# A hybrid attention step on one core: token tiles loaded first, constants on ScalarE's queue, the first chunks' high part straight from PSUM, and another order of modulation, turns and squares

## The chip, the core and the metric

One core of a Trainium2 chip runs the whole step as one program. Its engines are TensorE (PE; its weight loads are listed apart as PEld), VectorE (DVE), ScalarE (ACT), GpSimd (POOL) and SyncE (SP), each with its own queue of instructions that it works off in order; SP and ACT also issue the DMAs used here. The metric is the device time of one execution in microseconds. The kernel before takes 723.14 us, the median of three runs (722.96 to 723.36).

## What is computed

One layer of a diffusion backbone, for 128 context tokens and 1024 latent tokens of width 1024. Two attention branches (A global, B windowed) read one input projection; the change touches only what stands ahead of that projection: the modulated norm.

```python
shift, scale, gate = modulation(c, w_mod[l], b_mod[l])        # silu(c) @ w_mod + b_mod, split in three
h = rmsnorm(xs, norm_gain[l]) * (1.0 + scale) + shift          # 1024 latent tokens x 1024 columns
q_a, k_a, v_a, g_a, q_b, k_b, v_b, g_b = project(h, w_in[l], ...)
...
xs = xs + gate * merge_out(o_a, g_a, o_b, g_b, w_out[l])
```

The context tokens go the same way with a conditioning vector of their own (`c_ctx`).

## The kernel before

The projection needs h with its 1024 columns on the partitions, so h is made transposed, in eight **chunks** j of 128 columns. Nine token tiles of 128 rows (`xn`, tile 0 the context, 1 to 8 the latent tokens) are loaded by `load_x`, normed by `norm` (ACT squares and sums the tile, POOL makes `msx` and its power -1/2 `rsx`, DVE scales the tile by it in `scaled`), and turned on PE against the identity into a PSUM bank `px`. Two vectors per chunk, `a_mod` and `b_col`, hold scale and shift. They come from `modulate_rows(j)`: eight products of the Silu of the conditioning with the chunk's modulation weights `wm` (1 MB, three buffers, `load_wm`), copied out of PSUM as `mrows`; and `modulate(j)`: two turns of `mrows`, a reduction `m`, and two small operations on DVE. ACT then makes `hf` = px * a_mod + b_col (L401).

All products run in float32r with every operand split in a high and a low part: `h_at(0, ...)` is the rounded value of hf, made by a cast on DVE (L406), `h_at(1, ...)` is hf minus it, made on POOL (L407). The weights of the input projection are split alike by `split`: `whi` is cast on ACT (L233), `wlo` subtracted on DVE (L235), on POOL for every second chunk of the gate weights of branch B only. A product is high x high, high x low (`gate_high`, L262 and L263) and low x high (L258).

The first thing projected is branch A's gate (`W_GA`, raw chunks `rawga`, three buffers). Over tokens 1 to 4 (`first_gates`, four banks of 512 columns, one for each channel group ch) and 5 and 6 (`next_gates`, 256 columns, one chunk behind), the products run while the later chunks of h are still being made: the loop `for j in range(KT + 2)` makes chunk j and multiplies chunk j-1. Its pass j=0 is the opening: warm-up matmuls (`warm(n)`, a product of the identity with no use, n from `WARM`), the norms of tiles 1 to 6, the modulation of chunk 0. Tiles 7, 8 and 0 follow in the passes j=1 to 4.

The order of the work is the order of the source: at the end `in_order` chains every engine's instructions as written. PSUM banks for the turns alternate between two (`bank_tr`, tags D and E): the rows of a modulation and the transposes of a chunk take turns on them. Two engines that read the same bank are put one after the other. DMAs rotate over eight semaphores, so that an issue waits until the DMA issued eight places earlier has landed; a raw weight buffer is loaded again when its split is done, a `wm` buffer when its products are.

Of the kernel before, what the change touches and what calls it, by code (L numbers as in the profile page):

```python
# [18 lines left out]
P = 128  # L19
D = 1024  # L20
# [35 lines left out]
PAD = 2  # L56
X_FROM = 1
SECOND_FROM = 5
WARM = (8, 4, 4, 2)
WIDE = 5  # L60
LOADLEAD = 5
OUTRATE = 2.5
PADRATE = 3
POOL_LO = ("gb",)
NOG = 5
PES = 3
GATE_LATE = 2
# [40 lines left out]
def hybrid_step(ctx, tc, x_prompt, x_sample, cache_k_a, cache_v_a, cache_k_b, cache_v_b,  # L108
# [97 lines left out]
    class Weights:  # L206
# [22 lines left out]
        def split(self):  # L229
            k = len(self.hi)  # L230
            h = wp.tile([P, 512], F32R, tag="whi", name=f"whi{self.tag}_{k}")
            l = wp.tile([P, 512], F32R, tag="wlo", name=f"wlo{self.tag}_{k}")
            nc.scalar.copy(h, self.raw[k])  # L233
            eng = nc.gpsimd if self.tag in POOL_LO and k % 2 else nc.vector
            eng.tensor_tensor(l, self.raw[k], h, op=ALU.subtract)  # L235
            self.hi.append(h)
            self.lo.append(l)
            self.load()
# [71 lines left out]
    FIRST = [1, 2, 3, 4, 5, 6]  # L310
    with tc.tile_pool(name="st", bufs=2, side="right") as st:
        ident = st.tile([P, P], F32, name="ident", bufs=1)
        nc.sync.dma_start(ident, k_ident)
        nc.vector.tensor_copy(ident_r, ident)
        nc.vector.tensor_copy(ident_b, ident)
        nc.gpsimd.tensor_copy(diag, ident[0:4, 0:4])
        colt = st.tile([P, 48], F32, name="colt", bufs=1)
        nc.sync.dma_start(colt, cols)
        st.tile([P, 16], F32, name="pad3", bufs=1)

        def group_sum(out, eye):
            nc.vector.tensor_tensor(out, eye[:, 0:2], eye[:, 32:34], op=ALU.add)
            for a in (64, 96):
                nc.vector.tensor_tensor(out, out, eye[:, a : a + 2], op=ALU.add)

        wm = []

        def load_wm(j):
            w = st.tile([P, KT, 2, P], F32, tag="wm", name=f"wm{j}", bufs=3)
            nc.sync.dma_start(w, w_mod_ss[j])  # L330
# [15 lines left out]
        def modulate_rows(j):  # L346
            pm = pmod[j] = bank_tr(f"pm{j}")
            for k in range(KT):
                a = 32 * (k % 4)
                nc.tensor.matmul(pm[a : a + 32, 0:256], sil32[:, k, :], wm[j][:, k].rearrange("p s n -> p (s n)"),  # L350
                                 start=(k < 4), stop=(k >= 4), tile_position=(0, a))
            mrows[j] = st.tile([P, 256], F32, tag="mrows", name=f"mrows{j}")
            (nc.scalar.copy if j else nc.vector.tensor_copy)(mrows[j], pm[:, 0:256])

        def modulate(j):
            pm = pmod.pop(j)[:, 256:512]
# [6 lines left out]
            nc.vector.tensor_scalar(a_mod[:, j, :], m4[:, 0], bsc1[:, j : j + 1], colt[:, 16 + j : 17 + j],  # L363
                                    op0=ALU.add, op1=ALU.mult)
            nc.vector.tensor_scalar(b_col[:, j, :], m4[:, 1], colt[:, 24 + j : 25 + j], None, op0=ALU.add)

        xn = {}

        def load_x(t):
            xn[t] = st.tile([P, D], F32, name=f"xn{t}", bufs=1)  # L370
            nc.sync.dma_start(xn[t], x_tile[t])

        rx = {}

# [3 lines left out]
        def norm(t, now_=True):  # L378
# [10 lines left out]
            else:  # L389
                rx[t] = r  # L390

        def transposed(j, t0, n, cond):
            px = bank_tr(f"px{j}_{t0}")
            for i in range(n):
                if j == 0 and t0 == 1:
                    warm(WARM[3])
                nc.tensor.transpose(px[:, P * i : P * i + P], xn[t0 + i][:, P * j : P * j + P], ident)
# [3 lines left out]
            nc.scalar.activation(hf[:, :w], px[:, :w], AF.Identity,  # L401
                                 scale=a_mod[:, j, cond : cond + 1], bias=b_col[:, j, cond : cond + 1])
            step = w if third(dst) else 2 * P
            for o in range(0, w, step):
                i, to = third(slice(dst.start + o, dst.start + o + step))
                nc.vector.tensor_copy(h_at(0, i, j, to), hf[:, o : o + step])  # L406
                nc.gpsimd.tensor_tensor(h_at(1, i, j, to), hf[:, o : o + step], h_at(0, i, j, to), op=ALU.subtract)  # L407

        for t in FIRST[:4]:
            load_x(t)  # L410
        W_GA.load()
        load_x(5)
        load_x(6)
        load_wm(1)
        W_GA.load()
        load_wm(2)
        def warm(n):

            for _ in range(n):
                nc.tensor.matmul(small[0], ident_b, ident_b.unsqueeze(1).to_broadcast([P, 4, P]), start=True, stop=True)  # L420
# [19 lines left out]

        for j in range(KT + 2):
            if j == 0:
                warm(WARM[0])
                norm(1)
                modulate_rows(0)
                warm(WARM[1])
                norm(2)
                modulate(0)
                warm(WARM[2])
                norm(3)  # L450
                norm(4)
# [23 lines left out]
            if big_on:  # L475
                first_gates(2, j - 1)
            if j < KT:
                modulate(j)
                transposed(j, 1, 4, 0)
            if big_on:  # L480
                first_gates(3, j - 1)
            if j < KT:
                transposed(j, 5, 2 if j < WIDE else 4, 0)
# [839 lines left out]
```

## Time and profile before

| what | value |
|---|---|
| median of three runs | 723.14 us |
| the profiled execution: span from first to last instruction | 721.3 us |
| the median's part outside such a span | 1.84 us |
| granted TensorE clock, mean over the span | 0.993 |
| PE idle in the span (721.3 - 698.3 busy) | 23.0 us |
| DMA: bytes moved, mean | 78.56 MB, 109 GB/s |

The time of the profiled execution beside its span isn't recorded; the span and the median are set side by side here. Times in all rows are microseconds from the start of the span; a row of the timeline gives start, duration, engine, line, operation, output and inputs, count, and in brackets the idle time of the engine ahead of it with what ended it. A row of a stretch gives its length, then the busy time of PE, PEld, DVE, ACT and POOL with the number of instructions, the granted clock, the DMA engines' busy share and GB/s. A stretch asked for PE alone has PE's busy time alone. SPq and ACTq are the DMA issues of SP and ACT.

### The profile page before, as it was taken

Reading aid. Unit: us, or ns where it says so; the run is one execution under the profiler, and the core shown is the slowest. Engines: PE = TensorE matmul, PEld = TensorE weight load, DVE = VectorE, ACT = ScalarE, POOL = GpSimd, SP = SyncE. Lnnn points to the kernel's source line nnn. Section 1 sums busy time; section 2 is a strip of 40 time slices with the busy share of each in tenths; the row PEclk is TensorE's granted clock in tenths of the full one; section 3 lists DMA queues with packets and bytes.
Section 4 is the critical chain, followed back from the end, with each engine's and each line's share of the span. In section 5 each row is a group of like instructions: output and inputs, shape, how many; then the busy total and the mean of one; then the engine's idle time right before and its main releaser. Section 6 shows DMA issues by size and latency. Waiting matters only on the chain. (4 is left out here: it accounts for less than half of the span.)

```text
span 721.3 us, 10622 instructions
## 1 busy us (share of the span) xinstructions
PE 698.3 (97%) x3524; PEld 559.7 (78%) x3524; DVE 457.6 (63%) x1007; ACT 411.7 (57%) x829; POOL 335.3 (46%) x355
## 2 busy tenths in 40 slices
PE   5999999999999999999999999999999999999997
PEld 2678988877777788977788888888888888887865
DVE  3466147875675872745866677577666775775653
ACT  5355411411232451158778877877787778877770
POOL 3456013332322340236666555655575557555751
PEclk9999999999999999999999999999999999999999
DMA  8961373348435115440321222121212221212323
GB/s 344 346 219 59 121 278 86 79 94 276 121 85 142 45 60 171 139 143 23 103 67 45 73 67 88 44 81 52 87 54 59 66 87 45 81 53 87 103 65 119
DMA packets 53159, 78.56 MB, mean 109 GB/s; under 512 B 6569, under 2 KB 25449, under 8 KB 52081
## 3 DMA queue, kind: packets, MB, share of 16 engines
q1 hardware_dynamic: 44928, 65.96, 28.1%
q10 hardware_dynamic: 8176, 11.94, 6.3%
q8 instruction: 28, 0.46, 0.3%
q14 instruction: 27, 0.21, 0.1%
HBM read 58.69 MB, written 19.18 MB: 108 GB/s over the span
## 5 line engine op out<-in xcount | busy, mean ns | idle before, releaser
L1108 POOL TENSOR_TENSOR pl<-pe,ph 128x512 fp32r<-128x512 f32 x130 | 167.6, 1292 | 144.7 <-DVE nm L919 67.5
L859 DVE TENSOR_REDUCE mx<-pmx 128x1 f32<-128x384 f32 x192 | 101.4, 552 | 59.5 <-PE pmx L858 58.1
L1100 ACT ACTIVATE pe<-st 128x512 f32<-128x512 f32 x146 | 86.8, 594 | 28.0 <-PE st L1098 27.1
L1104 ACT CAST ph<-pe 128x512 fp32r<-128x512 f32 x146 | 90.6, 621 | 4.8
L1118 PE MATMUL pv<-ph,v_hi 128*128 128x512 f32 x208 | 83.2, 400 | 2.2 <-DVE spare L1142 2.2
L1121 PE MATMUL pv<-pl,v_hi 128*128 128x512 f32 x208 | 82.6, 397 | 0.0
L173 POOL TENSOR_TENSOR rs_q<-ms_q,mhalf 128x8 f32<-128x8 f32 x18 | 34.8, 1931 | 82.1 <-DVE ms_q L171 82.1
L1189 PE MATMUL po<-wo,ogh 128*128 128x512 f32 x216 | 72.5, 394 | 0.2 <-DVE yt L1196 0.2
L919 DVE CUSTOM_DVE_ANT_0 sn<-sn,mask,nsink 128x512 f32<-128x512 f32 (+1 forms) x64 | 46.3, 724 | 38.3 <-PE sn L916 36.5
L858 PE MATMUL pmx<-kha,qt 128*128 128x384 f32 x192 | 61.0, 363 | 0.4 <-ACT pen L905 0.2
L1097 PE MATMUL st<-qt,kha 128*128 128x512 f32 x144 | 58.3, 405 | 1.5 <-ACT pe L1100 0.8
L1098 PE MATMUL st<-qb,kla 68*128 68x512 f32 x144 | 57.6, 400 | 1.1 <-DVE qb L878 1.1
L1120 PE MATMUL pv<-ph,v_lo 128*64 128x512 f32 x146 | 57.9, 396 | 0.0
L1121 PEld LDWEIGHTS pv<-pl,v_hi 128*128 128x128 f32 x208 | 39.4, 189 | 16.7 <-issue 0.2
L905 ACT ACTIVATE pen<-sn,nm 128x512 f32<-128x512 f32 (+2 forms) x72 | 45.0, 626 | 6.5 <-DVE nm L919 3.1
L1093 ACT CAST ph<-st 128x512 fp32r<-128x512 f32 x62 | 36.4, 587 | 19.9 <-PE st L1092 18.7
L1118 PEld LDWEIGHTS pv<-ph,v_hi 128*128 128x128 f32 x208 | 39.4, 189 | 10.5 <-ACT ogh L1154 2.4
L1189 PEld LDWEIGHTS po<-wo,ogh 128*128 128x128 f32 x216 | 40.0, 188 | 6.8 <-DVE yt L1196 0.6
L1094 DVE TENSOR_TENSOR pl<-st,ph 128x512 fp32r<-128x512 f32 x62 | 42.5, 686 | 2.3 <-ACT ph L1093 1.5
L1189 PE MATMUL po<-wo,ogl 128*128 128x512 f32 x108 | 42.6, 394 | 0.0
L594 ACT ACTIVATE sqq<-pq 128x512 f32<-128x512 f32 x18 | 10.8, 599 | 53.3 <-DMA qd<-qo0q 14.4
L858 PEld LDWEIGHTS pmx<-kha,qt 128*128 128x128 f32 x192 | 35.5, 190 | 6.2 <-DVE mx L859 1.4
(216 smaller groups left out, 1700.2 us busy)
## 6 DMA issues: line engine op xcount, KB each, us to landing
qt<-qd SPq DMA_DIRECT2D x36, 256.0 KB, 3.1
wm<-in_w_mod_ss_dram SPq DMA_DIRECT2D x8, 1024.0 KB, 5.1
qd<-qo0q ACTq DMA_DIRECT2D x36, 128.0 KB, 2.4
qd<-qo1q ACTq DMA_DIRECT2D x36, 128.0 KB, 2.4
sgl<-gd SPq DMA_DIRECT2D x36, 128.0 KB, 2.1
out_dram<-yt SPq DMA_DIRECT2D x17, 256.0 KB, 2.1
xn<-in_x_sample_dram SPq DMA_DIRECT2D x8, 512.0 KB, 7.0
wg<-in_w_mod_g_dram SPq DMA_DIRECT2D x4, 1024.0 KB, 7.9
```

The costliest lines, as they stand in the source:

```text
L858: nc.tensor.matmul(pm[:, 0:384], lhs, kha[:, g, 3 * b : 3 * b + 3, :], start=True, stop=True)
L859: nc.vector.tensor_reduce(mx[:, h, b : b + 1], pm[:, 0:384], axis=AX.X, op=ALU.max)
L919: nc.vector.tensor_tensor_reduce(s, s, mask[:, m0 : m0 + n], -1.0, nsink[:, 4 * g + h : 4 * g + h + 1], op0=ALU.add, op1=ALU.min, accum_ou ...
L1097: nc.tensor.matmul(s, kh, qtile[i], start=True, stop=False)
L1098: nc.tensor.matmul(s, kl, qbtile[i], start=False, stop=True)
L1100: nc.scalar.activation(pe, s, AF.Exp)
L1104: nc.scalar.copy(ph, pe)
L1108: nc.gpsimd.tensor_tensor(pl, pe, ph, op=ALU.subtract)
L1118: nc.tensor.matmul(pv, two, ph, start=(b == 0), stop=False)
L1120: nc.tensor.matmul(pv[0:64, :], vl, ph, start=False, stop=False)
L1121: nc.tensor.matmul(pv, two, pl, start=False, stop=last)
L1189: nc.tensor.matmul(po[n], a, wo_parts[KT * n + k][lo], start=(k == KS[0] and p == 0), stop=(k == KS[-1] and p == 2))
```

## The change

- ident and colt (the conditioning, the gain and the biases) are issued from ACT's queue, and SP starts with the four token tiles, then wm0 in two halves, the first weights, wm1, the second weights, tiles 5 and 6, wm2.
- The opening turns each of the four tiles into the bank of chunk 0 as soon as it is scaled, with warm-up matmuls between, and only then does chunk 0's modulation; `turned` and `modulated` are the two halves of the old `transposed`.
- For chunks 0 and 1 of tokens 1 to 4, ACT writes the high part straight from PSUM (L412 of the kernel after), DVE makes hf from the same bank (L413) and the low part (L414); the cast on DVE and the subtraction on POOL are gone there.
- The low part of the first weight chunk is subtracted on POOL (`POOL_FIRST`), the copied rows of chunk 1 on DVE instead of ACT.
- Tiles 5 and 6 are squared in pass 1 instead of the opening, and scaled later; their transposes of chunks 0 and 1 share one bank in pass 2. In pass 1 the modulation stands ahead of the products of ch 2 and 3, in pass 2 the order is changed as the diff shows. From pass 3 on the order is the old one.

```diff
-WARM = (8, 4, 4, 2)
+WARM = (7, 4, 5, 4, 2, 8)
+POOL_FIRST = (("ga", 0),)
...
-            eng = nc.gpsimd if self.tag in POOL_LO and k % 2 else nc.vector
+            eng = nc.gpsimd if (self.tag in POOL_LO and k % 2) or (self.tag, k) in POOL_FIRST else nc.vector
...
-        nc.sync.dma_start(ident, k_ident)
+        nc.scalar.dma_start(ident, k_ident)
...
-        nc.sync.dma_start(colt, cols)
+        nc.scalar.dma_start(colt, cols)
...
+        for t in FIRST[:4]:
+            load_x(t)
         wm = []
 
         def load_wm(j):
             w = st.tile([P, KT, 2, P], F32, tag="wm", name=f"wm{j}", bufs=3)
-            nc.sync.dma_start(w, w_mod_ss[j])
+            for a in range(0, KT, KT if j else KT // 2):
+                b = a + (KT if j else KT // 2)
+                nc.sync.dma_start(w[:, a:b], w_mod_ss[j][:, a:b])
             wm.append(w)
 
-        load_wm(0)
...
-            (nc.scalar.copy if j else nc.vector.tensor_copy)(mrows[j], pm[:, 0:256])
+            (nc.scalar.copy if j > 1 else nc.vector.tensor_copy)(mrows[j], pm[:, 0:256])
...
+        def turned(px, j, t):
+            nc.tensor.transpose(px, xn[t][:, P * j : P * j + P], ident)
...
+        def modulated(px, j, t0, n, cond):
             w = P * n
             dst = slice(P * place(t0), P * place(t0) + w)
             hf = st.tile([P, 512], F32, tag="hf", name=f"hf{j}_{t0}", bufs=3)
-            nc.scalar.activation(hf[:, :w], px[:, :w], AF.Identity,
-                                 scale=a_mod[:, j, cond : cond + 1], bias=b_col[:, j, cond : cond + 1])
+            a, b = a_mod[:, j, cond : cond + 1], b_col[:, j, cond : cond + 1]
+            if j < 2 and t0 == 1:
+                i, to = third(dst)
+                nc.scalar.activation(h_at(0, i, j, to), px[:, :w], AF.Identity, scale=a, bias=b)
+                nc.vector.tensor_scalar(hf[:, :w], px[:, :w], a, b, op0=ALU.mult, op1=ALU.add)
+                nc.vector.tensor_tensor(h_at(1, i, j, to), hf[:, :w], h_at(0, i, j, to), op=ALU.subtract)
+                return
+            nc.scalar.activation(hf[:, :w], px[:, :w], AF.Identity, scale=a, bias=b)
...
-        for t in FIRST[:4]:
-            load_x(t)
+        load_wm(0)
+        W_GA.load()
+        load_wm(1)
         W_GA.load()
         load_x(5)
         load_x(6)
-        load_wm(1)
-        W_GA.load()
         load_wm(2)
...
             if j == 0:
-                warm(WARM[0])
-                norm(1)
+                px = bank_tr("px0_1")
+                for i in range(4):
+                    norm(1 + i)
+                    warm(WARM[i])
+                    turned(px[:, P * i : P * i + P], 0, 1 + i)
                 modulate_rows(0)
-                warm(WARM[1])
-                norm(2)
+                W_GA.split()
+                warm(WARM[4])
                 modulate(0)
-                warm(WARM[2])
-                norm(3)
-                norm(4)
-                W_GA.split()
-                norm(5)
-                transposed(0, 1, 4, 0)
-                norm(6)
-                load_wm(3)
+                modulated(px, 0, 1, 4, 0)
+                warm(WARM[5])
                 continue
             big_on, small_on = j <= KT, 2 <= j
             if j < KT:
                 W_GA.split()
+            if j == 1:
+                load_wm(3)
+                norm(5, False)
...
             if j == 1:
-                transposed(0, 5, 2, 0)
+                modulate(1)
+                scaled(5, rx.pop(5))
+                transposed(1, 1, 4, 0)
+                norm(6, False)
+                first_gates(2, 0)
+                first_gates(3, 0)
+            elif j == 2:
+                scaled(6, rx.pop(6))
+                px5 = bank_tr("px01_5")
+                for i in range(4):
+                    turned(px5[:, P * i : P * i + P], i // 2, 5 + i % 2)
+                modulate(2)
+                for i in range(2):
+                    modulated(px5[:, 256 * i : 256 * i + 256], i, 5, 2, 0)
+                first_gates(2, 1)
+                transposed(2, 1, 4, 0)
+                first_gates(3, 1)
+                transposed(2, 5, 2, 0)
+            else:
```

SP's queue at the start of the program, before:

```order
L313 DMA ident<-in_k_ident_dram 128x128
L318 DMA colt<-in_cols_dram 128x48
L330 DMA wm_169<-in_w_mod_ss_dram 128x2048
L371 DMA xn_178<-in_x_sample_dram 128x1024
L371 DMA xn_180<-in_x_sample_dram 128x1024
L371 DMA xn_182<-in_x_sample_dram 128x1024
L371 DMA xn_184<-in_x_sample_dram 128x1024
L221 DMA rawga_186<-in_w_in_dram 128x512
L371 DMA xn_188<-in_x_sample_dram 128x1024
```

and now:

```order
L331 DMA xn_169<-in_x_sample_dram 128x1024
L331 DMA xn_171<-in_x_sample_dram 128x1024
L331 DMA xn_173<-in_x_sample_dram 128x1024
L331 DMA xn_175<-in_x_sample_dram 128x1024
L341 DMA wm_184<-in_w_mod_ss_dram 128x1024 x2
L222 DMA rawga_187<-in_w_in_dram 128x512
L341 DMA wm_189<-in_w_mod_ss_dram 128x2048
L222 DMA rawga_191<-in_w_in_dram 128x512
L331 DMA xn_193<-in_x_sample_dram 128x1024
L331 DMA xn_195<-in_x_sample_dram 128x1024
```

The tiles moved ahead of 1 MB of modulation weights, the constants left this queue, and tiles 5 and 6 moved behind wm1 and the second weights.

ACT's queue from the square of the fourth tile (`sq`) to the high part of chunk 1, before:

```order
L382 ACTIVATE sq_261,ss_262<-xn_184 128x1024
L233 CAST whiga_269<-rawga_186 128x512
L382 ACTIVATE sq_275,ss_276<-xn_188 128x1024
L401 ACTIVATE hf_1_296<-px_1_283,b_col,a_mod 128x512
L382 ACTIVATE sq_300,ss_301<-xn_190 128x1024
L233 CAST whiga_310<-rawga_194 128x512
L353 COPY mrows_329<-pm_320 128x256
L401 ACTIVATE hf_5_340<-px_5_337,b_col,a_mod 128x256
L401 ACTIVATE hf_1_358<-px_1_353,b_col,a_mod 128x512
```

and now, up to the copied rows of chunk 2:

```order
L386 ACTIVATE sq_249,ss_250<-xn_175 128x1024
L234 CAST whiga_273<-rawga_187 128x512
L412 ACTIVATE h_0_0_115<-px_1_205,b_col,a_mod 128x512
L234 CAST whiga_299<-rawga_191 128x512
L386 ACTIVATE sq_307,ss_308<-xn_193 128x1024
L412 ACTIVATE h_0_1_116<-px_1_342,b_col,a_mod 128x512
L386 ACTIVATE sq_351,ss_352<-xn_195 128x1024
L234 CAST whiga_364<-rawga_277 128x512
L363 COPY mrows_383<-pm_374 128x256
```

The squares of tiles 5 and 6 moved from ahead of the two activations to behind each of them; that of tile 6 stands ahead of the cast of the third weights.

DVE's queue from the last scaled tile of the opening to the split of the second weights, before:

```order
L376 TENSOR_SCALAR xn_184<-xn_184,rsx_266 128x1024
L235 TENSOR_TENSOR wloga_270<-rawga_186,whiga_269 128x512
L376 TENSOR_SCALAR xn_188<-xn_188,rsx_280 128x1024
L406 CAST h_0_0_115<-hf_1_296 128x512
L376 TENSOR_SCALAR xn_190<-xn_190,rsx_305 128x1024
L235 TENSOR_TENSOR wloga_311<-rawga_194,whiga_310 128x512
```

and now, up to the scaling of tile 6:

```order
L414 TENSOR_TENSOR h_0_0_123<-hf_1_287,h_0_0_115 128x512
L236 TENSOR_TENSOR wloga_300<-rawga_191,whiga_299 128x512
L363 COPY mrows_327<-pm_318 128x256
L371 TENSOR_REDUCE m_1_337<-pm_318 128x4
L373 TENSOR_SCALAR a_mod<-m_1_337,bsc_178,colt 128x2
L375 TENSOR_SCALAR b_col<-m_1_337,colt 128x2
L380 TENSOR_SCALAR xn_193<-xn_193,rsx_312 128x1024
L413 TENSOR_SCALAR hf_1_347<-px_1_342,a_mod,b_col 128x512
L414 TENSOR_TENSOR h_0_1_124<-hf_1_347,h_0_1_116 128x512
L236 TENSOR_TENSOR wloga_365<-rawga_277,whiga_364 128x512
L380 TENSOR_SCALAR xn_195<-xn_195,rsx_356 128x1024
```

The low part of the first weights left the queue, the low parts of the first two chunks came in, and tile 6 is scaled behind the split of the third weights.

More of the change, by code (lines that the diff above doesn't have):

```diff
@@ L324, in group_sum, with load_x @@
                 nc.vector.tensor_tensor(out, out, eye[:, a : a + 2], op=ALU.add)
+        xn = {}
+        def load_x(t):
+            xn[t] = st.tile([P, D], F32, name=f"xn{t}", bufs=1)
+            nc.sync.dma_start(xn[t], x_tile[t])
+        for t in FIRST[:4]:
+            load_x(t)
         wm = []
@@ L365, in modulate @@
             nc.vector.tensor_scalar(b_col[:, j, :], m4[:, 1], colt[:, 24 + j : 25 + j], None, op0=ALU.add)
[L367 to L371, printed above, removed]
         rx = {}
@@ L394, in transposed @@
             for i in range(n):
-                if j == 0 and t0 == 1:
-                    warm(WARM[3])
-                nc.tensor.transpose(px[:, P * i : P * i + P], xn[t0 + i][:, P * j : P * j + P], ident)
+                turned(px[:, P * i : P * i + P], j, t0 + i)
+            modulated(px, j, t0, n, cond)
+        def modulated(px, j, t0, n, cond):
             w = P * n
@@ L473, in hybrid_step @@
             if j == 1:
-                transposed(0, 5, 2, 0)
[L475 to L483, printed above, removed]
+                modulate(1)
[17 more added lines that the diff above has]
+            else:
+                if big_on:
+                    first_gates(2, j - 1)
+                if j < KT:
+                    modulate(j)
+                    transposed(j, 1, 4, 0)
+                if big_on:
+                    first_gates(3, j - 1)
+                if j < KT:
+                    transposed(j, 5, 2 if j < WIDE else 4, 0)
             if X_FROM + 1 < j <= X_FROM + 4:
```

## The prediction

> **What bounds the kernel now.** I read the page's busy table and slices first, then the stretches of the first 40 us, the waits of those stretches, and the timeline around each wait.
>
> ```profile
> PE 698.3 (97%) x3524; PEld 559.7 (78%) x3524; DVE 457.6 (63%) x1007; ACT 411.7 (57%) x829; POOL 335.3 (46%) x355
> 0.00:17.47 17.47, 10.14 (x46) 3.78 (x46) 6.61 (x16) 9.51 (x16) 6.13 (x16) 1.00 0.87 341
> 31.60:37.90 6.30, 6.30 (x51) 4.82 (x50) 2.58 (x7) 3.16 (x7) 3.16 (x5) 1.00 0.81 292
> 25.30 0.50 PE L262 MATMUL pg_f<-h,whiga 128*128 128x512 f32 x1 [0.42 <-DVE h L406]
> 31.69 0.40 PE L262 MATMUL pg_f<-h,whiga 128*128 128x512 f32 x1
> 37.99 0.40 PE L262 MATMUL pg_f<-h,whiga 128*128 128x512 f32 x1
> ```
>
> PE is busy 97% of the span, and from the third chunk (j=3, first product at 31.69) a chunk is 6.30 us of PE work in 6.30 us. So an edit ahead of 31.69 is worth just the amount by which that product comes sooner; nothing behind it is edited. Ahead of it lie 17.47 us before the first real product, chunk one (17.47 to 25.30, 7.83 us) and chunk two (25.30 to 31.69, 6.39 us). These three numbers are what I recompute.
>
> ```profile
> 6.72 0.33 SPq L330 DMA_DIRECT2D wm<-in_w_mod_ss_dram  x1
> 8.00 0.33 SPq L221 DMA_DIRECT2D rawga<-in_w_in_dram  x1
> 11.77 0.33 SPq L330 DMA_DIRECT2D wm<-in_w_mod_ss_dram  x1
> 8.00 1.06 ACT L382 ACTIVATE sq<-xn 128x1024 bf16<-128x1024 f32 x1 [4.51 <-DMA xn<-in_x_sample_dram]
> 10.12 0.75 DVE L376 TENSOR_SCALAR xn<-xn,rsx 128x1024 f32<-128x1024 f32 x1 [6.35 <-POOL rsx L386]
> 11.79 1.06 ACT L382 ACTIVATE sq<-xn 128x1024 bf16<-128x1024 f32 x1
> 15.35 0.33 PE L397 MATMUL px<-ident,xn 128*128 128x128 f32 x1 [0.70 <-DVE xn L376]
> 15.71 0.78 ACT L401 ACTIVATE hf<-px,b_col,a_mod 128x512 f32<-128x512 f32 x1 [0.86 <-PE px L397]
> 17.00 0.42 DVE L406 CAST h<-hf 128x512 fp32r<-128x512 f32 x1
> 17.47 0.50 PE L262 MATMUL pg_f<-h,whiga 128*128 128x512 f32 x1 [1.80 <-DVE h L406]
> ```
>
> The first product hangs on the loads: SP issues a load only when the one eight places earlier has landed, so its rows date the landings. The first modulation weights (wm0, 1 MB) land near 6.7, the first token tile at 8.00, the fourth at 11.77: 1.26 us per 512 KB tile. ACT squares each tile as it lands; the fourth takes 11.79 to 15.35 to reach its transpose, and then hf on ACT, the cast on DVE, the product.
>
> **The change, step by step.** *Loads.* The token tiles now stand ahead of wm0 and their first issue moves to where ident's was.
>
> ```profile
> 0.72 0.40 SPq L313 DMA_DIRECT2D ident<-in_k_ident_dram  x1
> 1.64 0.42 SPq L330 DMA_DIRECT2D wm<-in_w_mod_ss_dram  x1
> 3.33 3.60 PE L420 MATMUL pg_s<-ident_b 128*128 128x512 bf16 x8 [3.33 <-DVE ident_b L315]
> ```
>
> The fourth tile loses 1 MB ahead of it (2 x 1.26 = 2.5 us) and starts 0.92 earlier, less about 0.2 for the 88 KB of ident and colt that now share the first microseconds: 11.77 - 3.25 = 8.5; the first lands at 8.5 - 3 x 1.26 = 4.7. By the same rate wm0 lands at 11.0, the first weight chunk 11.6, wm1 14.2, tiles five and six 16.1 and 17.3, wm2 19.9, the third weight chunk 20.5. ACT issues ident at the time SP did; its table load then ends near 2.9, and the Silu it delays is wanted only by wm0's products.
>
> *Transposes.* At before's pace (11.79 to 15.35) the fourth tile could be transposed at 12.1, the first at 4.7 + 2.87 + 0.1 = 7.7. But the warm-up matmuls stand in PE's queue between them, 7, 4, 5, 4, and here the clock decides.
>
> ```profile
> 1.87:5.29 3.42, 1.96 (x5) 1.00 0.78 246
> 5.29:8.70 3.41, 3.41 (x20) 1.00 1.00 406
> 18.94:22.35 3.41, 3.41 (x22) 0.50 1.02 423
> 8.72 1.04 PE L420 MATMUL pg_s<-ident_b 128*128 128x512 bf16 x4
> 18.59 1.66 PE L350 MATMUL pm<-wm,sil 128*32 128x256 f32 x16
> 26.42 1.07 PE L350 MATMUL pm<-wm,sil 128*32 128x256 f32 x16
> ```
>
> The granted clock is 0.50 from 18.94 to 22.35, a window of 3.41 us. The column says 1.00 at the start, yet the first eight warm-up matmuls take 3.60 us (0.43 each) against about 0.22 each in the row at 8.72. I read PE as slow until 8.70, a window edge: the window before it was busy throughout, the one before that for 1.96 of 3.42 (57%) and brought no release. Now the seven first ones end at 3.33 + 3.0 = 6.35 and PE idles until 7.7, so the window to 8.70 is busy 2.1 of 3.41, 62%. That row is unknown between 57% (no release) and 100% (release). Nearest is 57%, so I take no release at 8.70 but at 12.11. At 0.43 each, four end at 9.5, five at 11.75, and one slow and three fast at about 12.95; the fourth transpose runs there, not at 12.1. With release at 8.70 this 0.9 us is not paid.
>
> *Modulation moved behind the transposes.* It was hidden under the loads; now it is on the path.
>
> ```profile
> 10.79 0.42 DVE L353 COPY mrows<-pm 128x256 f32<-128x256 f32 x1
> 11.26 0.44 PE L359 MATMUL pm<-ident,mrows 128*128 128x128 f32 x2 [1.50 <-DVE mrows L353]
> 29.18 0.17 DVE L361 TENSOR_REDUCE m<-pm 128x4 f32<-128x16 f32 x1 [1.81 <-PE pm L359]
> 29.58 0.22 DVE L365 TENSOR_SCALAR b_col<-m,colt 128x2 f32<-128x2 f32 x1
> 29.92 1.23 ACT L401 ACTIVATE hf<-px,b_col,a_mod 128x512 f32<-128x512 f32 x2 [1.99 <-DVE b_col L365]
> ```
>
> From 13.1: products 1.07, copy 0.42, turns 0.44, reduce to b_col 0.62, ACT's activation 0.78 (now writing the high part itself), with 0.05 to 0.1 between: 16.7. Eight fast warm-ups behind the turns (15.1) end at 16.85, so **the first product comes at 16.85, 0.6 sooner**. DVE's cast (17.00 to 17.42 before, half a microsecond behind ACT's end at 16.49) is gone from this path. The low weight part goes to POOL: 1.29 us by the row below, from 12.3, done by 13.6, hidden.
>
> *Chunk one.* The kernel before had 3.41 us of it at half clock (1.7 lost), turned tiles five and six in it (four transposes, 0.45), and ended in the wait of 0.42 at 25.30.
>
> ```profile
> 17.50 1.29 POOL L407 TENSOR_TENSOR h<-hf,h 128x512 fp32r<-128x512 f32 x1 [1.20 <-DVE h L406]
> 33.72 0.72 PE L258 MATMUL pg_f<-h,whiga 128*128 128x512 f32 x2
> 35.20 0.60 PE L397 MATMUL px<-ident,xn 128*128 128x128 f32 x4
> L1094 DVE TENSOR_TENSOR pl<-st,ph 128x512 fp32r<-128x512 f32 x62 | 42.5, 686 | 2.3 <-ACT ph L1093 1.5
> ```
>
> Now hf from PSUM and the subtraction run on DVE behind ACT's read of the same bank: twice 0.69 by the row of L1094 (bounds 0.42, the cast, and 1.29, POOL). They end 1.4 us after the first product could start, while PE has 2.0 us of products (31.69 to 33.72) ahead of the low part: hidden. wm1's products take the bank that hf is read from; they come 1.03 in, DVE's read ends 0.5 in: hidden too, by half a microsecond. By the steady rows the chunk is 2.03 to the low products, 0.5 for them, 0.1 of waiting for the copied rows, 0.2 turns, 0.35 transposes, 1.4 for channels two and three: 4.6. Its successor needs the next high part at 2.85 + 0.1 + 0.62 + 0.1 + 0.78 + 0.1 = 4.55. I take 4.65, **3.2 less than 7.83**. PE is nearly idle-free from 12.95 on, so I see no reason for half clock.
>
> *Chunk two.* It gains four transposes (10 instead of 6, 0.45) and a new wait: ACT squares tile six, then casts weights, DVE splits them and only then scales tile six.
>
> ```profile
> 20.40 0.69 DVE L235 TENSOR_TENSOR wloga<-rawga,whiga 128x512 fp32r<-128x512 f32 x1
> 18.01 0.62 ACT L233 CAST whiga<-rawga 128x512 fp32r<-128x512 f32 x1 [0.48 <-DMA rawga<-in_w_in_dram]
> ```
>
> From the high part at chunk start -0.2: square 1.25, cast 0.62, split 0.69, scale 0.75, small gaps: 3.1 in; PE wants tile six at 2.6. So 0.5 of waiting; behind it stand all the products of the chunk. With 6.30: 7.25, **0.86 more than 6.39**. The chunk starts at 21.5, wants wm2 at 22.5 (lands 19.9) and the third weights at 22.6 (20.5): two microseconds of cover; if that goes, every further microsecond is paid. Other moved issues: wm3 waits for wm0's release at 14.2 and lands near 24, wanted at 30.
>
> Sum: -0.62 - 3.18 + 0.86 = -2.94. Span 721.3 - 2.9 = 718.4; the median, 723.14, has 1.84 outside the span, which stays: **720.2**.
>
> **Rivals.** *The clock comes at 8.70.* Then the fourth transpose is at 12.1 and everything behind it 0.9 to 1.0 sooner: 719.2. For it: 62% lies above 57%. Against: the one window here that met the slow clock with less than full work released nothing. The page "TensorE: Matmul & The Clock Gate" of the Trainium skill (Part 1) says that these windows run freely and do not start with the kernel; the trace's 3.41 us spacing agrees, and by that rule the release could fall elsewhere in each run, though the three times before lie within 0.40 us.
>
> *POOL is not ready.* Between its memset and its first mean, POOL has an instruction without a row (a reload of its library, one place ahead of the mean in both kernels).
>
> ```profile
> 2.82 0.30 POOL L342 MEMSET sil<- 128x256 f32 x1
> 9.24 0.19 POOL L384 TENSOR_SCALAR msx<-ss 128x1 f32<-128x1 f32 x1 [6.12 <-ACT sq L382]
> 10.53 0.39 POOL L384 TENSOR_SCALAR msx<-ss 128x1 f32<-128x1 f32 x1 [0.45 <-ACT sq L382]
> 11.00 0.56 POOL L386 TENSOR_TENSOR rsx<-msx,mhalf 128x1 f32<-128x1 f32 x1
> ```
>
> It lasts anything from nothing to 6.1 us, for the first mean started 0.09 after ACT's accumulator was read. Before, nothing needed POOL sooner; now ACT delivers at 6.0, so a load over 2.9 us is paid. At 6.1: first mean 9.2, four pairs of 1.03 end at 13.3, the first transpose at 10.9 after 4.5 us of idle PE; nine slow warm-ups reach 15.0, release at 15.53, fourth transpose 16.3, first product 20.1: 723.5. Released a window later (18.94), about 1.6 more with slow products: 725.1. Against it: the first mean follows ACT as promptly as the second (0.08), which a load ending just then would do only by chance. The Trainium skill's "GPSIMD Engine Reference" (2.1 Instruction dispatch) gives about 6 us for the first call into freshly loaded code, with no visible instruction; by that figure the load would end at 9.07, an estimate that this trace neither shows nor excludes, and the kernel would be the slower one.
>
> *The gain is handed back.* Loads over two microseconds later than the rows' rate, or another window at half clock further on (1.7 us), give 721.9 to 722.5. *The change does next to nothing*: modulation, 3.6 us, now stands behind the transposes. If the tiles came only 1.6 us sooner, the first product would be at 17.6, and if PE then met a half-clock window again (1.7), the gain would be -0.1 + 3.2 - 1.7 - 0.86 = 0.5: 722.6. The loads' rate and the eight warm-ups speak against it.
>
> **How the numbers follow.** Forecast 0.43 (719.7 to 720.9), early clock 0.27, handed back 0.13, nothing 0.05, POOL 0.12. The range leaves out POOL and some of the rest: 718.7 to 722.3. About 0.2%, 1.45 us, is what a measurement can tell from no change. Faster than 721.7: forecast, early clock and part of the third, 0.77. Within: 0.16, with POOL's mild half. Slower: 0.07.
>
> **What would show it.** Right: fourth transpose near 13, first product near 16.9, no 0.50 window before 30, third chunk's first product near 28.7, a wait of PE for xn in chunk two. Early clock: warm-ups of 0.22 from 8.70. Wrong: POOL's first mean much later than ACT's first square, or weights landing after 22.6.

## The result and the profile after

| | before | after |
|---|---|---|
| median, 20 runs of each | 723.14 us (721.93 to 726.99) | 721.65 us (721.15 to 723.39) |
| ratio | | 0.9976, 95% interval 0.9967 to 0.9985 |
| profiled execution: span, mean granted clock | 721.3 us, 0.993 | 720.4 us, 1.000 |
| first product of chunk one | 17.47 | 18.41 (forecast 16.85) |
| first product of chunk two | 25.30 | 23.25 (forecast 21.5) |
| first product of chunk three | 31.69 | 30.75 (forecast 28.75) |

The kernel after is 1.49 us faster, 0.24%; the forecast was 2.94. The profiled execution of after took 722.6 us, so it is one of the slower of the twenty, by 0.95 over their median. That has to be kept in mind with every row below.

The page of the kernel after: its span, and busy time by engine with the number of instructions.

```profile
span 720.4 us, 10635 instructions
PE 698.1 (97%) x3530; PEld 558.6 (78%) x3530; DVE 458.3 (64%) x1009; ACT 411.1 (57%) x828; POOL 335.4 (47%) x354
```

From chunk three on nothing has changed: the next chunk begins 6.29 us after 30.75, where before it was 6.30, and the lead of 0.94 is kept to the end of the span (0.9). So the whole result lies in the first 31 us, as the prediction had it. The timeline of the kernel after, its opening:

```profile
4.47 0.60 DVE L315 CAST ident_r<-ident 128x128 fp32r<-128x128 f32 x1 [3.62 <-DMA ident<-in_k_ident_dram]
4.84 0.48 SPq L341 DMA_DIRECT2D wm<-in_w_mod_ss_dram  x1
...
5.20 3.17 PE L433 MATMUL pg_s<-ident_b 128*128 128x512 bf16 x7 [5.20 <-DVE ident_b L316]
...
6.00 0.22 ACT L344 ACTIVATE silc<-colt 128x16 f32<-128x16 f32 x1 [3.07 <-DMA colt<-in_cols_dram]
...
6.12 1.04 ACT L386 ACTIVATE sq<-xn 128x1024 bf16<-128x1024 f32 x1
...
7.34 0.19 POOL L388 TENSOR_SCALAR msx<-ss 128x1 f32<-128x1 f32 x1 [2.35 <-ACT sq L386]
...
8.31 0.33 SPq L341 DMA_DIRECT2D wm<-in_w_mod_ss_dram  x1
...
9.74 1.06 ACT L386 ACTIVATE sq<-xn 128x1024 bf16<-128x1024 f32 x1
...
11.22 2.34 PE L433 MATMUL pg_s<-ident_b 128*128 128x512 bf16 x5
...
12.65 0.75 DVE L380 TENSOR_SCALAR xn<-xn,rsx 128x1024 f32<-128x1024 f32 x1 [0.72 <-POOL rsx L390]
...
14.56 0.27 PE L397 MATMUL px<-ident,xn 128*128 128x128 f32 x1
...
17.58 0.78 ACT L412 ACTIVATE h<-px,b_col,a_mod 128x512 fp32r<-128x512 f32 x1 [4.84 <-DVE b_col L375]
18.39 0.81 DVE L413 TENSOR_SCALAR hf<-px,a_mod,b_col 128x512 f32<-128x512 f32 x1 [0.91 <-ACT h L412]
18.41 0.50 PE L263 MATMUL pg_f<-h,whiga 128*128 128x512 f32 x1
```

Read it from the loads down. SP's row at 8.31 waited for the fourth tile and dates its landing, for which the forecast was 8.5. The row at 4.84 follows straight on SP's issue before it (4.46), so it only bounds the landing of the first tile: by 4.84, forecast 4.7. The tiles came on time. But ACT does not square the first tile until 6.12, at least 1.3 us after it has landed. Its queue says why: the Silu of the conditioning (L344) stands ahead of the squares, and it waited 3.07 us for colt, until 6.00. The four squares then follow one another at ACT's own pace, 1.2 us each, so the fourth starts at 9.74 and not at 8.5; its tile is scaled by 13.40. There PE is not ready either: warm-up matmuls at half rate (five in 2.34 us) hold it until 14.56. From there on the chain runs as it was forecast, 3.85 us to the first product (forecast 3.9).

PE's busy time in the clock's windows of the kernel after (stretch, its length, PE busy, granted clock, DMA share, GB/s):

```profile
7.00:10.41 3.41, 2.74 (x8) 1.00 1.01 333
10.41:13.82 3.41, 3.41 (x10) 1.00 1.03 426
13.82:17.23 3.41, 3.40 (x28) 1.00 1.05 428
```

Matmuls turn fast at 13.82. The window from 7.00 was busy for 2.74 of 3.41 us (80%) and brought no release; the full one behind it did. The column says 1.00 throughout, as at the start of the kernel before; the rate of the warm-up matmuls is the better witness.

Chunk two of the kernel after, in the timeline:

```profile
23.03 1.04 ACT L386 ACTIVATE sq<-xn 128x1024 bf16<-128x1024 f32 x1
...
23.25 0.43 PE L263 MATMUL pg_f<-h,whiga 128*128 128x512 f32 x1
...
25.84 0.75 DVE L380 TENSOR_SCALAR xn<-xn,rsx 128x1024 f32<-128x1024 f32 x1 [0.45 <-POOL rsx L390]
...
26.65 0.55 PE L397 MATMUL px<-ident,xn 128*128 128x128 f32 x3 [0.50 <-DVE xn L380]
...
29.23 0.36 PE L263 MATMUL pg_s<-h,whiga 128*128 128x256 f32 x1
...
30.75 0.40 PE L263 MATMUL pg_f<-h,whiga 128*128 128x512 f32 x1
```

The new wait is there with the size that was forecast, 0.50 us, on the scaling of tile six. What was late is another link, though: the split of the third weights ended at 25.39 and DVE then stood idle for 0.45, waiting for POOL's power (`rsx`).

### The profile page after: what moved, and what is told of

It is laid out like the page before. It is cut to its first block, busy times and chain, and to the rows that moved or that the text cites. A ratio compares the mean times of both kernels' runs of the same rounds, so it can differ in the third digit from the quotient of the medians.

```text
span 720.4 us, 10635 instructions
## 1 busy us (share of the span) xinstructions
PE 698.1 (97%) x3530; PEld 558.6 (78%) x3530; DVE 458.3 (64%) x1009; ACT 411.1 (57%) x828; POOL 335.4 (47%) x354
```

## The experiments

Each is an edit of the kernel after, but the last, which edits the kernel before. Ratios are to the kernel before, run on the same chip in the same batch (medians there 723.08, 723.11 and 722.85). The kernel after was not run again beside them, so a difference from its 721.65 is one between batches.

**Constants back ahead of the tiles, on SP.** This undoes one part: ident and colt are early again, and the tiles 0.92 us later.

```diff
-        nc.scalar.dma_start(ident, k_ident)
+        nc.sync.dma_start(ident, k_ident)
...
-        nc.scalar.dma_start(colt, cols)
+        nc.sync.dma_start(colt, cols)
```

> The changed kernel with one part undone: ident and colt are again issued on SP's queue, ahead of the token tiles. Theory A (the two constants, issued beside the tiles, land late and hold ACT at the Silu and PE at its first warm-up): ident lands near 2.6 instead of 4.5, colt near 3.3 instead of 5.95, the first warm-up starts near 3.3 instead of 5.2; the first tile lands 0.6 to 0.9 later (5.5 to 5.7) and is squared at once, 0.4 to 0.6 sooner than the 6.12 of the changed kernel; first product 17.3 to 17.9 instead of 18.41; 0.5 to 1.1 us less than the changed kernel. Rival B (the squares waited for the tiles, not for colt): the first square comes at 6.8 or later and the time is 0.5 to 0.9 us more. Rival C (only the warm-up matmuls and the clock set the opening): the squares don't matter, the first product moves with the first warm-up by up to 1.9.

721.40 us, ratio 0.9982 (0.9969 to 0.9995): 0.25 below the kernel after, no gain that the runs can tell. Its squares in the timeline, first, third and fourth:

```profile
5.23 1.06 ACT L386 ACTIVATE sq<-xn 128x1024 bf16<-128x1024 f32 x1 [2.10 <-DMA xn<-in_x_sample_dram]
...
9.02 1.06 ACT L386 ACTIVATE sq<-xn 128x1024 bf16<-128x1024 f32 x1 [1.21 <-DMA xn<-in_x_sample_dram]
...
10.26 1.06 ACT L386 ACTIVATE sq<-xn 128x1024 bf16<-128x1024 f32 x1
```

The Silu ran at 2.90 here, and the squares begin as the first tile lands. But now they wait for tiles (1.21 us for the third), and the fourth starts at 10.26, later than the 9.74 of after. In this profile the first product came at 17.30, 1.11 sooner than in the profile of after and inside the range of theory A; but the clock was released at 11.05 here and at 13.82 there, so the two profiles do not price the constants alone, and the medians bear out no such gain. The constants cost something in either place: on SP the tiles land later (the fourth square starts 0.52 later), on ACT the Silu waits. Whether the Silu must stand ahead of the squares is the next question.

**The Silu behind the squares.** The loads stay as in after; the Silu and its two followers go behind the four norms, and a Silu of a constant pulls ACT's table load ahead.

```diff
-        nc.scalar.activation(silc, colt[:, 0:16], AF.Silu)
+        nc.scalar.activation(dummy, mhalf, AF.Silu)
...
+                condition()
                 modulate_rows(0)
```

> The changed kernel with the Silu of the conditioning, the sum bsc1 and the copy into sil32 moved behind the four squares and scalings (a Silu of eight constants ahead of them keeps the table load where it was); the constants stay on ACT's queue. Theory A: the first square starts at 4.9 instead of 6.12, the fourth at 8.4 to 8.6 instead of 9.74, the fourth tile is scaled by 12.2 instead of 13.4; its transpose is then held by the slow warm-up matmuls alone, 12.3 to 13.6 by the clock's window; first product 16.3 to 17.6; 0.8 to 1.6 us less. Rival B: first square stays at 6.1 and nothing moves. Rival C: the squares come sooner but the fourth transpose stays at 14.3, since the warm-ups from 5.2 on set it. POOL's reload: if it lasts over 1 us the first mean comes later than 0.1 behind the first square's sum.

720.69 us, ratio 0.9963 (0.9948 to 0.9978), 0.96 us below the kernel after, although the two intervals overlap. The timeline of this kernel shows the mechanism by itself:

```profile
4.59 1.06 ACT L392 ACTIVATE sq<-xn 128x1024 bf16<-128x1024 f32 x1 [1.45 <-DMA xn<-in_x_sample_dram]
...
8.63 1.06 ACT L392 ACTIVATE sq<-xn 128x1024 bf16<-128x1024 f32 x1
...
9.68 0.20 ACT L356 ACTIVATE silc<-colt 128x16 f32<-128x16 f32 x1
...
11.94 0.33 PE L403 MATMUL px<-ident,xn 128*128 128x128 f32 x1 [0.28 <-DVE xn L386]
...
15.85 0.50 PE L263 MATMUL pg_f<-h,whiga 128*128 128x512 f32 x1
```

The squares now start with the landings (4.59, and the fourth at 8.63, where 8.5 was forecast), and the Silu waits for nothing. The clock was released at 8.28 in this execution. The prediction's rival of an early clock put the fourth transpose at 12.1 and the first product 0.9 to 1.0 ahead of 16.85; the rows say 11.94 and 15.85.

**Fewer warm-up matmuls between the transposes**, on top of the last one.

```diff
-WARM = (7, 4, 5, 4, 2, 8)
+WARM = (7, 1, 1, 1, 2, 8)
```

> As the run before it, with one warm-up matmul instead of four, five and four ahead of the second, third and fourth transposes. Theory A with slow warm-ups as a cost of their own: the fourth transpose follows its tile at once, 12.2 to 12.4, and the first product comes near 16.2 where the clock has been released by then; if the thinner work leaves the clock slow, chunk 0's modulation products take 1.7 to 1.9 instead of 1.07, the first product comes near 17 and a part of chunk one runs at half speed (up to 1.7 us more), so the time is between 1.5 less and 0.5 more than the changed kernel. Theory that warm-ups cost nothing: the same first product as in the run before.

721.17 us, ratio 0.9978 (0.9964 to 0.9991): not better than 720.69, and not told apart from it. In its profile PE idles for 0.92 us ahead of the fourth transpose (11.68), which hangs on the tile's chain and not on PE, and the first product comes at 15.58, 0.27 sooner than in the run before it. So between these transposes the warm-ups cost little once they run at full rate. Only 2 of its 12 runs have a mean clock of 0.9985 or more, as 2 of 11 have in the run before it; that thinner warm-ups delay the release in other executions is not shown.

**The cast back on the path of the high part.**

```diff
-            if j < 2 and t0 == 1:
+            if False:
```

> The changed kernel with one part undone: chunks 0 and 1 of the first four token tiles go again through hf on ACT, the cast on DVE and the subtraction on POOL. If the direct high part is on the path: first product 0.4 to 0.6 later (18.9), chunk one 0.4 to 0.6 longer, 0.9 to 1.2 us more in all. If it was hidden: no change.

722.58 us, ratio 0.9994 (0.9981 to 1.0007): 0.93 above the kernel after, where the ends of the two intervals just overlap. The timeline, from the fourth transpose to the first product, and the first product of tokens 5 and 6 (`pg_s`):

```profile
13.25 0.33 PE L397 MATMUL px<-ident,xn 128*128 128x128 f32 x1 [0.28 <-DVE xn L380]
...
17.13 0.43 DVE L420 CAST h<-hf 128x512 fp32r<-128x512 f32 x1 [0.91 <-ACT hf L416]
...
17.61 0.50 PE L263 MATMUL pg_f<-h,whiga 128*128 128x512 f32 x1 [0.32 <-DVE h L420]
...
28.83 0.36 PE L263 MATMUL pg_s<-h,whiga 128*128 128x256 f32 x1
```

4.36 us here and 3.85 in the kernel after; and from the first product to the first of `pg_s` it takes 11.22 us instead of 10.82 (18.41 to 29.23). So the direct high part is worth about 0.9, half of it on the path to the first product and the rest in chunks one and two.

**Tile six squared one step earlier**, ahead of chunk 1's high part and the third weights in ACT's queue.

```diff
                 norm(5, False)
+                norm(6, False)
...
-                norm(6, False)
```

> The changed kernel with one line moved: the square of tile six stands right behind that of tile five on ACT, ahead of the high part of chunk one. If PE's wait of 0.50 for tile six in chunk two is this square's place: the wait goes (tile six is scaled 1 us sooner), chunk two takes 7.0 instead of 7.5 and the time falls by 0.5; the high part of chunk one isn't later, since ACT has 2 us idle ahead of it. Rival: tile six or the third weights land too late, or the high part is pushed back: the wait stays or moves to the first product of chunk two, and nothing is won.

721.96 us, ratio 0.9983 (0.9972 to 0.9994). In its timeline tile six is scaled ahead of the need, and all four transposes run without a wait:

```profile
24.26 0.74 DVE L380 TENSOR_SCALAR xn<-xn,rsx 128x1024 f32<-128x1024 f32 x1
...
24.91 0.69 PE L397 MATMUL px<-ident,xn 128*128 128x128 f32 x4
...
27.64 0.36 PE L263 MATMUL pg_s<-h,whiga 128*128 128x256 f32 x1
```

From the first product (17.45) to the first of `pg_s` it is 10.19 us instead of 10.82, 0.63 less. The medians do not show it against after (721.96 and 721.65), where a fall by 0.5 was expected. Nor do runs alike in their clock: the 10 of 12 here with a mean clock under 0.9985 have a median of 721.96, the 10 of 20 such runs of after 721.98. So the gain is seen in the trace alone. The same edit **together with the Silu behind the squares**:

> The Silu behind the four squares and tile six squared early, together. If the two costs are separate, they add: first product near 15.9 where the clock comes as early as in the run with the Silu last, third chunk's first product 0.5 sooner than in that run, median 720.69 - 0.5 = 720.2. Rival: the weights for chunk two land near 20 and now hold it, and only a part of the 0.5 is won.

720.22 us, ratio 0.9957 (0.9942 to 0.9973), lowest to highest 719.82 to 721.12. That is 0.47 under the run with the Silu alone, as expected, but with six runs and intervals that overlap for most of their length. Its trace shows what the rival expected, a part of the gain lost again, though in the next chunk. Chunk two takes 6.86 us instead of 7.52 in the run with the Silu alone, but chunk three 6.66 instead of 6.29:

```profile
27.42 0.40 PE L263 MATMUL pg_f<-h,whiga 128*128 128x512 f32 x1
...
29.03 1.06 ACT L392 ACTIVATE sq<-xn 128x1024 bf16<-128x1024 f32 x1 [2.22 <-DMA xn<-in_x_sample_dram]
...
30.60 0.36 ACT L369 COPY mrows<-pm 128x256 f32<-128x256 f32 x1
31.02 0.44 PE L375 MATMUL pm<-ident,mrows 128*128 128x128 f32 x2 [0.15 <-ACT mrows L369]
...
34.08 0.40 PE L263 MATMUL pg_f<-h,whiga 128*128 128x512 f32 x1
```

ACT now waits for the load of tile seven, and the copied rows that PE needs stand behind that tile's square: once more a wait in ACT's queue that holds what is queued behind it.

**Warm-up matmuls on a tile that is set by DVE**, so that they need no ident and begin at once; on top of the last one.

```diff
+        busy = st.tile([P, P], BF16, name="busy", bufs=1)
+        nc.vector.memset(busy, 1.0)
...
-WARM = (7, 4, 5, 4, 2, 8)
+WARM = (15, 4, 5, 4, 2, 8)
```

> As the run before it, with the warm-up matmuls on a tile of ones that DVE sets at once instead of on the identity, so that they don't wait for a DMA, and 15 instead of 7 ahead of the first transpose. Theory that the clock is released at the end of a window of 3.41 us that is (nearly) full of work, wherever the windows lie: warm-ups start near 1.3 and run until 7.5, so a full window ends at 8.1 at the latest, all later warm-ups take 0.22, the fourth transpose follows its tile (11.7 to 12.1), and the spread of the runs shrinks: median 719.6 to 720.1, and fewer runs above it by a microsecond. Rival (the release depends on something else, or the spread comes from later in the kernel): same median and spread as the run before it.

719.65 us, ratio 0.9955 (0.9939 to 0.9971), the lowest median of all, though not told apart from the run before it; four of its six runs lie between 719.2 and 719.7. The median came out as expected, the smaller spread did not: 719.22 to 721.67, against 719.82 to 721.12. Its timeline:

```profile
1.07 6.34 PE L441 MATMUL pg_s<-busy 128*128 128x512 bf16 x15 [1.07 <-DVE busy L316]
...
4.26 1.06 ACT L394 ACTIVATE sq<-xn 128x1024 bf16<-128x1024 f32 x1 [1.11 <-DMA xn<-in_x_sample_dram]
...
5.50 0.19 POOL L396 TENSOR_SCALAR msx<-ss 128x1 f32<-128x1 f32 x1 [0.53 <-ACT sq L394]
...
11.60 0.33 PE L405 MATMUL px<-ident,xn 128*128 128x128 f32 x1 [0.28 <-DVE xn L388]
```

The clock was released at 7.05. The first product came at 15.51, 0.21 sooner than in the run before it, but chunk three took 6.86 us here: ACT waits 2.42 us for the same load, and the lead is lost there.

**What the eight warm-ups behind the turns do.** After these runs one thing was open. The forecast had counted 1.7 us for a half-clock window in chunk one, which the profiled execution of before met; how often other executions meet it wasn't known. The records of each run's mean clock gave a hint: of 75 runs of the kernel before in the three batches, the 21 with a mean clock of 0.9985 or more took 721.97 us in the median (721.40 to 722.48), the other 54 took 723.21 (722.73 to 726.42). It is no more than a hint: the mean does not tell where a window lay, and it does not count a late release, ahead of which the column reads 1.00 (the profiled execution of after has a mean of 1.000 and took 722.6). PE's window ahead of that half-clock window in the kernel before was this:

```profile
15.53:18.94 3.41, 1.61 (x13) 1.00 1.02 423
```

It was busy for 47% of its time, because PE waits there for the first high part. The kernel after fills that wait with eight warm-up matmuls. Two kernels ask whether that matters: the kernel after without them, and the kernel before with them.

```diff
-WARM = (7, 4, 5, 4, 2, 8)
+WARM = (7, 4, 5, 4, 2, 0)
```

> The kernel after without the eight warm-up matmuls behind the turns of chunk 0 (they compute nothing that is used). Theory W: these eight keep PE busy while the modulation is finished, and so keep away the half-clock window that the kernel before met at 18.94 us behind a window busy only 47% of the time. Without them PE idles 1.5 to 2.0 us ahead of the first product; in those runs where a window edge makes that idle time its main part, chunk one falls to half clock. Then fewer runs than the 10 of 20 of the kernel after keep a mean clock of 0.9985 or more (4 or 5 of about 12), the median rises by 0.4 to 1.0 us to 722.1 to 722.7, and the runs at full clock stay near 721.4. Rival: the eight do nothing (the kernel after is free of half clock in chunk one because the rest of its opening is denser, or by luck): median 721.4 to 721.9, the share of full-clock runs as in the kernel after.

```diff
                 transposed(0, 1, 4, 0)
+                warm(8)
                 norm(6)
```

> The kernel before with eight more warm-up matmuls, put behind the transposes of chunk 0, ahead of the first product; nothing else is changed. They start at 15.7 and end near 17.5, when the first product was due, so they cost at most 0.2 us. Theory W: more than half of the change's gain of 1.49 us is the half-clock window in chunk one that 38 of 52 runs of the kernel before seem to have met somewhere (median 723.33 against 722.0 for the 14 at a mean clock of 0.9985 or more). With the eight, most runs keep the clock there: median 722.0 to 722.5, 0.6 to 1.1 us less than 723.1. Rival: the half-clock windows of the kernel before lie elsewhere, or another condition brings them: median 722.9 to 723.4, within 0.2 us of the kernel before.

Without them: 722.29 us, ratio 0.9993 (0.9983 to 1.0004), 0.64 above the kernel after, or 0.93 when each is set against the kernel before in its own batch; the five of twelve runs with a mean clock of 0.9985 or more have a median of 721.48, as such runs of after have (721.44). With them in the kernel before: 722.10 us, ratio 0.9991 (0.9982 to 0.9999), 0.75 under the kernel before beside it, and its slowest run took 722.65 where that took 724.94. Both medians came out as the theory of the window had them. By them, eight matmuls whose results nobody reads hold about half of the gain of the whole change.

The clocks did not all come out: more runs should keep a mean clock of 0.9985 or more with the eight, but it was 3 of 11 with them in the kernel before against 7 of 23 beside it, and 10 of 20 against 5 of 12 in the kernel after. What changed is the price of a lower mean clock. With the eight, runs under 0.9985 are slower than the others by 0.2 us in the kernel before and 0.54 in the kernel after; without them by 1.06 and 1.16. That fits half-clock windows that still come, but at cheaper places; where each run met its window is not on record, so for the medians this stays an argument. Where no window is lost, the change is worth less: 721.97 us before against 721.44 after, for the 10 of its 20 runs with a mean clock of 0.9985 or more. Timelines, first of the kernel after without them, with PE's window in that profile, then of the kernel before with them:

```profile
13.32 0.33 PE L397 MATMUL px<-ident,xn 128*128 128x128 f32 x1 [0.28 <-DVE xn L380]
...
17.23 0.50 PE L263 MATMUL pg_f<-h,whiga 128*128 128x512 f32 x1 [1.59 <-ACT h L412]
```

```profile
15.53:18.94 3.41, 1.82 (x17) 1.00 1.04 435
```

```profile
15.58 1.89 PE L420 MATMUL pg_s<-ident_b 128*128 128x512 bf16 x8
17.54 0.50 PE L262 MATMUL pg_f<-h,whiga 128*128 128x512 f32 x1
...
24.21 0.50 PE L262 MATMUL pg_f<-h,whiga 128*128 128x512 f32 x1 [0.53 <-DVE h L406]
```

In the first PE waits 1.59 us ahead of the first product. Its window has the same edges as the one above, was busy for 53% of its time instead of 47%, and no half clock followed it; so this profile does not show the window that the theory expects in other executions. It also tells what after's opening gives with a prompt clock, since its warm-up matmuls were fast by 9.06: first product at 17.23. In the second the eight end when the first product is due and delay it by less than 0.1 us. No half clock came, and chunk one of the old order takes 6.67 us (17.54 to 24.21) where it took 7.83 with the window: in the traces the window costs 1.16.

## Why the prediction was right or wrong

**The number: inside the range, partly by its width.** 721.65 lies in 718.7 to 722.3, but between the band of the forecast (719.7 to 720.9) and that of the gain handed back (721.9 to 722.5). The way was right, the gain half of what was told.

**What bounds it: right.** The lead of 0.94 us at chunk three's first product stayed to the end of the trace. Over the nine profiles with the same code behind that product, though, the rest of the span takes 688.8 to 690.1 us, so one pair of spans alone would not show such a lead.

**Loads: right**, by 4.84 for 4.7 and 8.31 for 8.5.

**The first product is the term that was mis-sized**: forecast 0.62 sooner, measured 0.94 later. The step that failed is the sentence on the constants: "its table load then ends near 2.9, and the Silu it delays is wanted only by wm0's products". That names who reads the Silu's result and leaves out who stands behind it in ACT's queue: the squares of all four tiles. The 0.2 us allowed for ident and colt was taken as a delay of the tiles; the small transfers were the ones delayed, ident by 1.9 us and colt by 2.7. The size can be read from three profiles. With the Silu out of the way and the clock at 8.28 the first product came at 15.85; with the Silu ahead and the clock by 9.06, at 17.23, so the Silu costs 1.38 (that profile lacks the eight warm-ups, which end as the first product is due); with the clock at 13.82, at 18.41, another 1.18. The forecast had held 15.9 and 0.95 for a late clock, which is right in kind.

**Chunk one: right in size**, 4.84 for 4.65, 7.83 before; no half-clock window came before 30 us. But the 7.83 is that of an execution with such a window. Without one the old order takes 6.67, so of the 2.99 in the traces 1.83 are the new order and 1.16 the window, which the forecast counted at 1.7. How much of the 1.16 reaches the median is a matter of how often the window comes; the two kernels with and without the eight warm-ups put it at 0.64 and 0.75.

**Chunk two: right**, 7.50 for 7.25, with the wait of 0.50 as forecast; removing it gave back 0.63 in the trace.

**The sum.** By the traces it is 0.94 - 2.99 + 1.11 = -0.94, against -2.94. By the medians 1.45 us are missing. The largest part is the Silu: the median with it behind the squares is 0.96 lower. A third of a microsecond is bookkeeping: the forecast put 1.84 outside the span by setting a profiled span against the median of other runs, while runs that list both have about 2.08 there before and 2.17 after. These two leave under 0.2, but that they close the account is partly luck. The forecast also took the window at 1.7, too much, and a late clock at 0.95 as paid by every execution, while three other profiles of this opening were released at 9.40, 10.15 and 8.70. These two errors pull in opposite directions, and no run separates them.

**The clock.** "The three times before lie within 0.40 us" was used against a release that differs between runs, and was wrong: twenty runs of before spread over 5 us. The nine kernels profiled before the last two were released at 8.70, 13.82, 11.05, 8.28, 10.10, 9.40, 10.15, 9.24 and 7.05, at no common place within 3.41 us. The Trainium skill says in "TensorE: Matmul & The Clock Gate", Part 1, that these windows run freely and do not start with the kernel; the traces agree. It also puts the return to half rate behind an idle window; here it followed one that was busy 47% of its time, and by the measurement idle is too strict a word.

**POOL: the rival fell.** Its first mean, at 7.34, started 0.09 us after ACT's sums were there, and POOL had been free for 2.35 us; in the kernel with warm-ups on a tile set by DVE it started at 5.50, 0.53 after the memset. The load of some 6 us that the Trainium skill gives in "GPSIMD Engine Reference" (2.1 Instruction dispatch) does not show at this place in any run here.

**The change does next to nothing, or hands the gain back:** neither came as told. Nothing of the loads was late, and no new half-clock window came into the opening.

## What to carry to other kernels

When a small load moves to another queue, ask of the instruction that waits for it not only who reads its result but what is queued behind it on its engine. Before a stall in one profiled execution goes into a sum, find out in how many runs it occurs; here the mean clocks of many runs gave a hint and two more kernels a price, where one profile could give neither. When the start of a chain comes sooner, look again at the loads that the later chunks wait for: tile seven's was hidden until the two waits ahead of it were gone. An idle stretch of PE ahead of dense work can cost twice, once as the wait and once as a window at half clock behind it, and matmuls without a use are a cheap cover if they need no late operand.

## What the hardware did that was not expected

- Small transfers issued on ACT's queue beside 512 KB tiles on SP's came late: ident, 64 KB, issued at 0.72, was there at 4.45 (in the kernel before at 2.6), and colt, 24 KB, issued at 1.18, only by 6.00 (before by 3.27), when the Silu ran. The tiles lost almost nothing: the fourth was there at 8.31.
- A window at half clock can follow one that is partly busy. Between 312 and 319 us, windows with 57 to 62% of PE's time busy were followed by one at 0.50 in five of the nine profiles, while windows of 58% near 232 us were not; ahead of and in the first chunks 47% was followed by one, 53% (the kernel after without the eight) and 56% (8.70 to 12.11 in the kernel before) were not. The busy share of the profile therefore isn't exactly what the clock goes by. In the opening a window of 80% brought no release, ones of 82 to 87% did.
